# Index queries of a sparse-attention layer projected and scored from position 64 on, with the first block's scores on 64 partitions

## The chip, the cores and the metric

One core of a Trainium2 chip runs the whole kernel in one launch. The metric is the device time of an execution in microseconds (us). Each engine has a queue of its own and works through it in order: TensorE (PE, with PEld for its weight loads), VectorE (DVE), ScalarE (ACT), GpSimd (POOL), and SyncE (SP), which issues transfers.

## The reference, cut to what matters

Two layers, each a token mixer and a gated MLP, over 256 positions of width 2048. Group B of the mixer is sparse attention: 16 index heads of 64 score the keys, and each query keeps the 64 best causal keys (`top_k` is 64 here).

```
q_idx = apply_rope(q_idx.reshape(bsz, s, IDX_HEADS, IDX_DIM), icos, isin)
top_k = min(INDEX_TOPK, s // 4)
...
    dots = jnp.einsum('bthd,bsd->bths', qi_b, k_idx, preferred_element_type=jnp.float32) * (IDX_DIM ** -0.5)
    index = jnp.einsum('bths,bth->bts', jax.nn.relu(dots), wi_b)
    index = jnp.where(visible[None], index, -jnp.inf)
    _, sel = lax.top_k(index, top_k)
    ...
    ok = (sel <= q_pos[None, :, None])[:, :, None, :]
    p = jax.nn.softmax(jnp.where(ok, logits, -jnp.inf), axis=-1)
```

A query at a position below 64 sees at most 64 keys, so it keeps all of them whatever their scores are. Group A of the mixer is a gated DeltaNet, which needs, for each layer, the inverse of unit triangular matrices built from its keys.

## The kernel before, in words

Everything is kept feature-major: a tile of x is 128 features by 256 positions. Matmuls run in fp32r with a split into a high and a low part: `X[:, k, :]` holds the high part of feature tile k in columns 0 to 255 and the low part in columns 256 to 511, and each weight chunk of 128 x 1024 is split into `hi` (ACT, L171) and `lo` (DVE, L173). Such a chunk is called a **unit** below: it holds eight feature tiles ("k tiles") of one output tile, so an output tile of an input projection takes two units. Per k tile, `mm3` issues either two matmuls (L219: hi times 512 columns; L221: lo times 256 columns) or, "folded", three of 256 columns into one half bank (L216).

A generator program interleaves the rest: after each unit of matmuls every open chain (`chain_k`, `chain_iq`, `chain_inverse` and so on) is stepped once or so, and what it issues is put into the engines' queues by the tile framework's scheduler. `lo` of a unit is issued some three units ahead of its matmuls. All of it is a fixed order at run time: an instruction that waits in DVE's queue holds up every `lo` behind it, and PE waits for `lo`.

The order of units in a layer's projections is: 8 units of a group (small columns and keys 0 to 2), keys 3 to 7, z of heads 0 and 1, **the eight index-query tiles (16 units, 128 k tiles, folded)**, z 2 to 5, the key-value latent, z 6 and 7, then v, q and attention queries by head. Counted through the program, the units' `lo` conversions of layer 0 are numbers 24 to 39 for the index queries.

Three chains matter here:

- `chain_iq(i)`: rotates an index tile of two heads (`rope`, L930 to L933), splits it (L1044 ACT, L1046 DVE), scores it against the keys with three matmuls for each block of 128 queries (L1059), takes the relu (ACT, L1061) and adds it up with the heads' weights into `idx` (DVE, L1066).
- `chain_topk`: eight rounds of max and match_replace on `idx`, then the mask `bias`.
- `chain_inverse`: once all eight heads' `LT` are written (DVE, L716), POOL issues the transfers that gather the diagonal blocks (L728, L732), then runs the first 16 steps of a substitution, each one product `Wd` (L749) and one subtraction into `BX` (L751). Steps 16 to 30 run on DVE with the same two lines; the first of them, on a product of 255 elements, is called **Wd255** below, and the last subtraction **BX31**. Then the result goes out and in through DRAM (L757, L766) and the merges for v can begin.

```
eng = nc.gpsimd if j < INV_POOL else V
eng.tensor_tensor(w, B[:, j, j + 1:32][:, :, None].to_broadcast([64, n, m]),
                   X[:, j:j + 1, 0:m].to_broadcast([64, n, m]), op=ALU.mult)
eng.tensor_tensor(X[:, j + 1:32, 0:m], X[:, j + 1:32, 0:m], w, op=ALU.subtract)
if j % IRATE == IRATE - 1:
    yield
```

Of the kernel before, what the change touches and what calls it, by code (L numbers as in the profile page):

```python
# [61 lines left out]
TOPK = 64  # L62
ROPE_THETA = 10000.0
# [9 lines left out]
# the tiles of the merges: (row block, (chunk, block, number of blocks))  # L73
# [9 lines left out]
for _n, _w in (("ident", 128), ("tri", 128), ("dmask", 128), ("bd", 128), ("cmask", 384),  # L83
               ("cos", 256), ("sin", 256), ("icos", 256), ("isin", 256), ("tcos", 128), ("tsin", 128)):
    CST[_n] = (_o, _o + _w)
    _o += _w
# [8 lines left out]
class Trunk:  # L95
# [161 lines left out]
    def single(self, src, xs, nk, done, pre=None, urgent=False, fold=False, sums=False):  # L257
        box = {}

        def unit(c0, n):  # L260
            def mm(hi, lo):
                if c0 == 0:
                    box["acc"] = self.newacc()
                for q in range(n):
                    if sums and c0 + n == nk and q == LNQ:
                        self.st = [self.bank("st"), self.bank("st")]
                        for st in self.st:
                            self.nc.tensor.matmul(st[:, 0:2], self.ones, self.zero, start=True, stop=False,
                                                  skip_group_check=True)
                    self.mm3(box["acc"], hi, lo, q, xs(c0 + q), c0 + q == 0, c0 + q == nk - 1, fold)  # L270
# [199 lines left out]
    def ln_out(self, l):  # L470
        # the last norm
# [87 lines left out]
    def chain_small(self, l, acc):  # L559
# [11 lines left out]
        # log decay and beta  # L571
# [14 lines left out]
        V.tensor_scalar(self.widx, tok[:, :, 80:96], 1.0 / 32, None, op0=ALU.mult)  # L586
        yield
# [20 lines left out]
        # cumulative decays  # L608
# [29 lines left out]
        # E[j, i] = exp(gc_i - gc_j) for i >= j  # L638
# [81 lines left out]
    def chain_inverse(self, l):  # L720
# [3 lines left out]
        # diagonal 32-blocks to one block a partition  # L724
# [8 lines left out]
        # the second chunk's blocks above the diagonal into the first one's room below it  # L733
# [4 lines left out]
        # norms of k  # L738
# [186 lines left out]
    def rope(self, dst, u, cosn, sinn):  # L925
        nc = self.nc
        V = nc.vector
        t = self.m256("rt")
        sn = self.c(sinn)
        V.tensor_tensor(t[0:64], u[64:128], sn[64:128], op=ALU.mult)  # L930
        V.tensor_tensor(t[64:128], u[0:64], sn[0:64], op=ALU.mult)  # L931
        V.tensor_tensor(dst, u, self.c(cosn), op=ALU.mult)
# [99 lines left out]
    def chain_iq(self, l, i, acc):  # L1032
        nc = self.nc
        V = nc.vector
        if FOLD & 2:
            u = acc[:, 0:256]
        else:
            u = yield from self.evac(acc, self.m256("u"))
            yield
        q = self.m256("iq")  # L1040
        self.rope(q, u, "icos", "isin")
        yield
        qh = self.m256("qh").bitcast(F32R)
        nc.scalar.activation(qh, q, AF.Copy)  # L1044
        ql = self.m256("ql").bitcast(F32R)
# [4 lines left out]
        for b in range(2):  # L1050
            n = P * (b + 1)
            o = (0, P)[b]
            for _ in range(YPD if b == 0 else YPD2):
                yield
            pd = self.bank("pd")
            pdv = pd[:, 0:2 * n].rearrange("p (w s) -> p w s", w=2)
            bs = slice(b * P, (b + 1) * P)
# [3 lines left out]
            nc.scalar.activation(rl[:, 0:2 * n], pd[:, 0:2 * n], AF.Relu)  # L1061
            yield
            for w in range(2):
                hh = 2 * i + w
                prev = self.c("cmask")[:, o:o + n] if i == 0 and w == 0 else self.idx[:, o:o + n]
                V.scalar_tensor_tensor(self.idx[:, o:o + n], rl[:, w * n:(w + 1) * n], self.widx[:, b, hh:hh + 1],  # L1066
                                       prev, op0=ALU.mult, op1=ALU.add)
# [5 lines left out]
    def chain_topk(self, l):  # L1073
# [11 lines left out]
        V.tensor_scalar(self.bias, self.idx, MARK, -NEG, op0=ALU.is_equal, op1=ALU.mult)  # L1085
        V.scalar_tensor_tensor(self.bias, self.bias, NEG, self.c("cmask"), op0=ALU.add, op1=ALU.add)
# [52 lines left out]
    def plan_layer(self, l):  # L1139
# [38 lines left out]
        for i in range(8):  # L1178
            nxt(lambda acc, i=i: sp(self.chain_iq(l, i, acc)), 2)
# [111 lines left out]
def _constants():  # L1291
# [12 lines left out]
    put("cmask", np.concatenate([cm, np.zeros((P, P)), cm], 1))  # L1304

# [94 lines left out]
```

## Time and profile before

| | us |
|---|---|
| Runs, median of 3 | 2493.53 (2491.78 to 2494.53) |
| Span of the profiled execution | 2492.8 |
| PE busy in it | 2441.6 (98%) |
| DVE busy | 1934.6 (78%) |
| ACT busy | 1236.9 (50%) |
| POOL busy | 285.5 (11%) |

The span runs from the first to the last instruction; the profiled execution has no other time of its own on record, so the span stands for it. PE's busy time counts overlapping matmuls once and includes their pipeline, so 98% doesn't mean that nothing can be gained on it. Layer 0's projections lie in the first 380 us, layer 1's between about 1240 and 1650 us; the two MLPs lie between and behind.

### The profile page before, as it was taken

How to read it: one execution, taken by the hardware profiler on the slowest of the kernel's cores; microseconds unless marked ns; L12 is line 12 of the kernel's file. 1: busy time of each engine (PE TensorE's matmuls, PEld its weight loads, DVE VectorE, ACT ScalarE, POOL GpSimd, SP SyncE). 2: the span in 40 equal slices, each digit the busy share in tenths (PEclk: the TensorE clock that was granted, in tenths of full speed). 3: DMA queues.
4: the chain of work that ended last, by engine and by line, in shares of the span. 5: the costliest groups of instructions: out<-in, count | busy, mean ns of one | idle time of the engine just before them, and what ended most of it. 6: DMA issues, size and time to landing. Idle time of an engine off the chain costs nothing.

```text
span 2492.8 us, 40103 instructions
## 1 busy us (share of the span) xinstructions
PE 2441.6 (98%) x15016; PEld 2171.0 (87%) x15016; DVE 1934.6 (78%) x3769; ACT 1236.9 (50%) x2137; POOL 285.5 (11%) x377
## 2 busy tenths in 40 slices
PE   9999999999999999999999999999999999999997
PEld 9997888898888888888899888888888888888886
DVE  7789988798888887555589798887888888875555
ACT  5445666454444444444354456664544444444443
POOL 0133101320000000000233221024100000000001
PEclk9999999999999999999999999999999999999998
DMA  7554445465555555666555644454555555555664
GB/s 243 182 172 135 137 147 159 150 196 186 187 191 188 188 187 188 185 186 188 158 189 160 174 133 130 152 163 150 193 187 190 188 189 186 190 186 182 187 187 133
DMA packets 135778, 436.29 MB, mean 175 GB/s; under 512 B 26624, under 2 KB 26912, under 8 KB 135328
## 3 DMA queue, kind: packets, MB, share of 16 engines
q1 hardware_dynamic: 134272, 429.14, 54.1%
q0 software_dynamic: 1312, 4.61, 0.7%
q8 instruction: 117, 1.92, 0.3%
q14 instruction: 77, 0.63, 0.1%
HBM read 429.61 MB, written 3.69 MB: 174 GB/s over the span
## 4 chain that ended last, share of the span: by engine, by line
PE 82%; DVE 12%; DMA 2%; issue 1%; ACT 1%; POOL 1%; SPq 0%; ACTq 0%; DVEq 0%; POOLq 0%
PE acc L219 46%; PE acc L221 24%; PE acc L216 6%; DVE lo L173 4%; PE acc L241 3%; DVE y L520 1%; DMA raw<-w_in 1%; ACT hi L171 1%; DMA G<-gd 1%; DVE YB L302 1%; POOL BX L751 0%; DVE rt L931 0%; DVE idx L1083 0%; PE pd L1059 0%; DVE idx L1066 0%
## 5 line engine op out<-in xcount | busy, mean ns | idle before, releaser
L219 PE MATMUL acc<-X,hi 128*128 128x512 f32 x4000 | 1418.3, 396 | 0.0
L173 DVE TENSOR_TENSOR lo<-raw,hi 128x1024 fp32r<-128x1024 f32 (+1 forms) x821 | 993.6, 1211 | 430.5 <-ACT hi L171 428.4
L171 ACT ACTIVATE hi<-raw 128x1024 fp32r<-128x1024 f32 (+1 forms) x821 | 853.7, 1040 | 868.9 <-PE acc L219 527.2
L221 PE MATMUL acc<-X,lo 128*128 128x256 f32 x4000 | 1121.7, 280 | 4.3 <-DVE lo L173 4.3
L219 PEld LDWEIGHTS acc<-X,hi 128*128 128x128 f32 x4000 | 751.1, 188 | 173.7
L221 PEld LDWEIGHTS acc<-X,lo 128*128 128x128 f32 x4000 | 751.3, 188 | 7.1 <-DVE lo L173 6.5
L219 PE MATMUL acc<-H,hi 128*128 128x512 f32 x1320 | 466.9, 396 | 0.0
L221 PE MATMUL acc<-H,lo 128*128 128x256 f32 x1320 | 372.2, 282 | 0.0
L219 PEld LDWEIGHTS acc<-H,hi 128*128 128x128 f32 x1320 | 248.0, 188 | 60.2
L216 PE MATMUL acc<-X,hi 128*128 128x256 f32 x1408 | 259.6, 284 | 0.6 <-ACT hi L171 0.6
L221 PEld LDWEIGHTS acc<-H,lo 128*128 128x128 f32 x1320 | 247.9, 188 | 0.1
L216 PEld LDWEIGHTS acc<-X,hi 128*128 128x128 f32 x1408 | 220.1, 190 | 2.1 <-ACT hi L171 0.8
L216 PE MATMUL acc<-X,lo 128*128 128x256 f32 x704 | 200.9, 285 | 9.1 <-DVE lo L173 9.1
L216 PEld LDWEIGHTS acc<-X,lo 128*128 128x128 f32 x704 | 133.4, 189 | 10.4 <-DVE lo L173 10.3
L376 POOL COPY racc<-xT 128x256 f32<-128x256 f32 x4 | 2.1, 527 | 1043.6 <-DVE xT L374 1043.6
L390 POOL TENSOR_TENSOR racc<-racc,xT 128x256 f32<-128x256 f32 x56 | 54.9, 981 | 496.8 <-DVE xT L386 496.7
L1255 ACT ACTIVATE sq<-y 128x256 f32<-128x256 f32 x88 | 36.7, 417 | 138.3 <-DVE y L520 138.2
L313 DVE TENSOR_TENSOR u<-acc,c 128x256 f32<-128x256 f32 x232 | 96.3, 418 | 0.3
L520 DVE SCALAR_TENSOR_TENSOR vT<-u,pv,vT 128x255 f32<-128x255 f32 (+1 forms) x176 | 85.1, 483 | 5.9
L520 DVE SCALAR_TENSOR_TENSOR y<-u,fw,y 128x255 f32<-128x255 f32 (+1 forms) x176 | 84.5, 480 | 2.9
L311 ACT ACTIVATE c<-acc 128x256 f32<-128x256 f32 x232 | 84.0, 366 | 4.6 <-PE acc L221 4.6
L241 PE MATMUL acc<-X,hi 128*128 128x256 f32 x512 | 78.1, 295 | 1.9 <-ACT hi L171 1.6
(324 smaller groups left out, 2136.7 us busy)
## 6 DMA issues: line engine op xcount, KB each, us to landing
raw<-w_up SPq DMA_DIRECT2D x336, 512.0 KB, 3.7
raw<-w_in SPq DMA_DIRECT2D x188, 512.0 KB, 3.7
raw<-w_down SPq DMA_DIRECT2D x160, 512.0 KB, 3.6
raw<-w_out SPq DMA_DIRECT2D x48, 512.0 KB, 3.7
raw<-w_out_g SPq DMA_DIRECT2D x16, 512.0 KB, 3.6
raw<-w_up_g SPq DMA_DIRECT2D x16, 512.0 KB, 4.1
raw<-w_down SPq DMA_DIRECT2D x32, 256.0 KB, 3.5
raw<-w_in_g SPq DMA_DIRECT2D x15, 512.0 KB, 4.6
```

Of the source, the lines that this page charges most:

```text
L171: nc.scalar.activation(u.hi[:, o:e], u.raw[:, o:e], AF.Copy)
L173: self.pin(nc.vector.tensor_tensor(u.lo[:, o:e], u.raw[:, o:e], u.hi[:, o:e].bitcast(F32), op=ALU.subtract))
L216: nc.tensor.matmul(acc[:, 0:256], w[:, j * P:(j + 1) * P], xs[:, o:o + 256], start=first and n == 0, stop=last and n == 2)
L219: nc.tensor.matmul(acc[:, 0:512], hi[:, j * P:(j + 1) * P], xs[:, 0:512], start=first, stop=last, skip_group_check=True)
L221: nc.tensor.matmul(acc[:, 256:512], lo[:, j * P:(j + 1) * P], xs[:, 0:256], start=False, stop=last, skip_group_check=True)
L241: self.nc.tensor.matmul(accs[f][:, 0:256], w[:, j * P:(j + 1) * P], xs(k)[:, o:o + 256], start=k == 0 and n == 0, stop=k == nk - 1 and n == 2)
L302: nc.vector.tensor_scalar(dst, src, scale, None, op0=ALU.mult)
L311: nc.scalar.activation(c, acc[:, 256:512], AF.Copy)
L313: nc.vector.tensor_tensor(u, acc[:, 0:256], c, op=ALU.add)
L390: nc.gpsimd.tensor_tensor(self.racc[:, 0, :], self.racc[:, 0, :], x, op=ALU.add)
L520: nc.vector.scalar_tensor_tensor(y[:, s:256], u[:, 0:256 - s], w[:, nt - 1 - s:nt - s], y[:, s:256], op0=ALU.mult, op1=ALU.add)
L1255: nc.scalar.activation(th, y, AF.Tanh)
```

## The change

Index queries for positions 0 to 63 are neither projected nor scored. `mm3` gets a start position `t0`; with it a k tile takes two matmuls, the high weights on columns 64 to 255 of both halves (384 columns) and the low weights on 192 columns. This replaces the folded form in the index tiles, so the two halves lie apart in the bank and `chain_iq` first copies one half (ACT) and adds it to the other (DVE), with a step between. Rotation and split work on 192 columns. The first block's scores (positions 64 to 127) lie on partitions 0 to 63, with a mask `cmaskq` and weights `widx0` moved there; the rounds of the top-k run on 64 partitions for that block, and `bias` is built in five operations instead of two, back on partitions 64 to 127. Constants grow by 128 columns.

```diff
-    def mm3(self, acc, hi, lo, j, xs, first, last, fold=False):
-        nc = self.nc
+    def mm3(self, acc, hi, lo, j, xs, first, last, fold=False, t0=0):
+        nc = self.nc
+        if t0:
+            nc.tensor.matmul(acc.rearrange("p (s t) -> p s t", s=2)[:, :, t0:256], hi[:, j * P:(j + 1) * P],
+                             xs.rearrange("p (s t) -> p s t", s=2)[:, :, t0:256], start=first, stop=last,
+                             skip_group_check=True)
+            nc.tensor.matmul(acc[:, 256 + t0:512], lo[:, j * P:(j + 1) * P], xs[:, t0:256], start=False, stop=last,
+                             skip_group_check=True)
+            return
...
+        self.widx0 = self.mp.tile([P, 16], F32, name="widx0")
+        V.tensor_scalar(self.widx0[0:P - Q0], tok[Q0:P, 0, 80:96], 1.0 / 32, None, op0=ALU.mult)
...
-        if FOLD & 2:
-            u = acc[:, 0:256]
-        else:
-            u = yield from self.evac(acc, self.m256("u"))
-            yield
-        q = self.m256("iq")
-        self.rope(q, u, "icos", "isin")
-        yield
-        qh = self.m256("qh").bitcast(F32R)
+        n0 = 256 - Q0
+        c = self.t256("c", 4)[:, 0:n0]
+        nc.scalar.activation(c, acc[:, 256 + Q0:512], AF.Copy)
+        yield
+        u = self.m256("u")[:, 0:n0]
+        V.tensor_tensor(u, acc[:, Q0:256], c, op=ALU.add)
+        yield
+        q = self.m256("iq")[:, 0:n0]
+        self.rope(q, u, "icos", "isin", Q0)
+        yield
+        qh = self.m256("qh").bitcast(F32R)[:, 0:n0]
...
+            r = P - Q0 if b == 0 else P
...
-            pdv = pd[:, 0:2 * n].rearrange("p (w s) -> p w s", w=2)
-            bs = slice(b * P, (b + 1) * P)
+            pdv = pd[0:r, 0:2 * n].rearrange("p (w s) -> p w s", w=2)
+            bs = slice(0, P - Q0) if b == 0 else slice(P - Q0, 256 - Q0)
...
-            vs = [self.idx[:, 0:P], self.idx[:, P:384]]
+            vs = [self.idx[0:P - Q0, 0:P], self.idx[:, P:384]]
...
-            nxt(lambda acc, i=i: sp(self.chain_iq(l, i, acc)), 2)
+            nxt(lambda acc, i=i: sp(self.chain_iq(l, i, acc)), t0=Q0)
```

Since the scheduler sets the queues anew, other instructions move too. On DVE, in layer 0, this is the place of the first DVE step of the inverse (`Wd` is the product, `BX` the matrix that it updates, `lo` a unit's conversion, `rt`, `iq`, `ql` and `idx` belong to the index chains), before the change:

```order
L933 TENSOR_TENSOR iq<-iq,rt 128x256
L1066 SCALAR_TENSOR_TENSOR idx<-rl,widx,idx 128x256 x2
L1046 TENSOR_TENSOR ql<-iq,qh 128x256
L749 TENSOR_TENSOR Wd<-BX 64x255
L173 TENSOR_TENSOR lo<-raw,hi 128x1024
L751 TENSOR_TENSOR BX<-BX,Wd 64x15x17
L749 TENSOR_TENSOR Wd<-BX 64x252
L930 TENSOR_TENSOR rt<-acc,cst 64x256
```

In the changed kernel the same place on DVE reads (line numbers are some 11 higher):

```order
L1058 TENSOR_TENSOR ql<-iq,qh 128x192
L175 TENSOR_TENSOR lo<-raw,hi 128x1024
L1050 TENSOR_TENSOR u<-acc,c 128x192
L760 TENSOR_TENSOR Wd<-BX 64x255
L762 TENSOR_TENSOR BX<-BX,Wd 64x15x17
L760 TENSOR_TENSOR Wd<-BX 64x252
L940 TENSOR_TENSOR rt<-u,cst 64x192
L762 TENSOR_TENSOR BX<-BX,Wd 64x14x18
L941 TENSOR_TENSOR rt<-u,cst 64x192
L942 TENSOR_TENSOR iq<-u,cst 128x192
L760 TENSOR_TENSOR Wd<-BX 64x247
L175 TENSOR_TENSOR lo<-raw,hi 128x1024
```

What moved: counted from the program's start, Wd255 stood behind 44 `lo` conversions and now stands behind 40; in layer 1 it stood behind 453 and now stands behind 450. BX31 stood behind 51 and 459, and now stands behind 48 and 458. The norm step of the same chain, just behind the last `LT`, stood behind 34 and 444 and now stands behind 32 and 442.

On PE, this is a piece of the index tiles of layer 0 before the change, around a score matmul (`pd`):

```order
L216 MATMUL acc<-X,hi 128x256
L1059 MATMUL pd<-pair_1116,qh 128x256
L1059 MATMUL pd<-pair_1117,qh 128x256
L1059 MATMUL pd<-pair_1116,ql 128x256
L216 MATMUL acc<-X,hi 128x256
L216 MATMUL acc<-X,lo 128x256
L216 MATMUL acc<-X,hi 128x256 x2
```

And in the changed kernel, around the first score matmul of a 64-query block on PE:

```order
L217 MATMUL acc<-X,hi 128x2x192
L220 MATMUL acc<-X,lo 128x192
L1072 MATMUL pd<-pair_1098,qh 64x256
L1072 MATMUL pd<-pair_1099,qh 64x256
L1072 MATMUL pd<-pair_1098,ql 64x256
L217 MATMUL acc<-X,hi 128x2x192
```

What moved: two matmuls, of 384 and 192 columns, stand where three of 256 stood, and the scores keep their columns but write 64 partitions.

## Rows read from the trace of the kernel before

**Rows 1.** The page: span, and busy time, share and instructions of PE.

```profile
span 2492.8 us, 40103 instructions
...
PE 2441.6 (98%) x15016; PEld 2171.0 (87%) x15016; DVE 1934.6 (78%) x3769; ACT 1236.9 (50%) x2137; POOL 285.5 (11%) x377
```

**Rows 2.** Timeline of PE in an index unit: start us, duration us, instruction.

```profile
126.36 0.40 PE L216 MATMUL acc<-X,hi 128*128 128x256 f32 x2
...
126.72 0.40 PE L216 MATMUL acc<-X,hi 128*128 128x256 f32 x2
```

**Rows 3.** Timeline of PE in the MLP, units not folded.

```profile
800.14 0.28 PE L221 MATMUL acc<-X,lo 128*128 128x256 f32 x1
800.26 0.39 PE L219 MATMUL acc<-X,hi 128*128 128x512 f32 x1
800.49 0.28 PE L221 MATMUL acc<-X,lo 128*128 128x256 f32 x1
```

**Rows 4.** Timeline of PE: attention logits, plain fp32, two passes a matmul.

```profile
235.89 0.39 PE L1106 MATMUL pl<-ak,iq 128*128 128x128 f32 x2
236.11 0.60 PE L1107 MATMUL pl<-ak,iq 128*128 128x256 f32 x2
236.54 0.38 PE L810 MATMUL p<-F,us 128*128 128x128 f32 x2
```

**Rows 5.** Timeline of PE: matmuls of one moving column, each with its weights.

```profile
480.81 0.58 PE L398 MATMUL st<-inv,xT 128*128 128x1 f32 x4
481.26 0.47 PE L398 MATMUL st<-inv,sq 128*128 128x1 f32 x3
```

**Rows 6.** Timeline of POOL, layer 0: the inverse's first issue, first and last instruction.

```profile
104.86 2.60 POOL L728 DMA_DIRECT2D d<-LT  x4 [43.18 <-DVE rs_q L326]
...
118.28 0.23 POOL L749 TENSOR_TENSOR Wd<-BX 64x31 f32<-64x31 f32 x1 [6.06 <-DMA BX<-d]
...
143.82 0.80 POOL L751 TENSOR_TENSOR BX<-BX,Wd 64x256 f32<-64x256 f32 x1
```

**Rows 7.** Timeline of POOL, layer 1: its last instruction of the inverse.

```profile
1379.75 0.72 POOL L751 TENSOR_TENSOR BX<-BX,Wd 64x256 f32<-64x256 f32 x1
```

**Rows 8.** Timeline of DVE, layer 0: conversion 41, Wd255, BX31, conversion 52.

```profile
131.13 1.65 DVE L173 TENSOR_TENSOR lo<-raw,hi 128x1024 fp32r<-128x1024 f32 x1
...
145.68 0.41 DVE L749 TENSOR_TENSOR Wd<-BX 64x255 f32<-64x255 f32 x1
...
167.00 0.17 DVE L751 TENSOR_TENSOR BX<-BX,Wd 64x31 f32<-64x31 f32 x1
...
168.47 1.21 DVE L173 TENSOR_TENSOR lo<-raw,hi 128x1024 fp32r<-128x1024 f32 x1
```

**Rows 9.** Timeline of DVE, layer 1: conversion 451, Wd255, BX31.

```profile
1368.21 1.65 DVE L173 TENSOR_TENSOR lo<-raw,hi 128x1024 fp32r<-128x1024 f32 x1
...
1380.51 0.42 DVE L749 TENSOR_TENSOR Wd<-BX 64x255 f32<-64x255 f32 x1 [4.23 <-POOL BX L751]
...
1401.99 0.18 DVE L751 TENSOR_TENSOR BX<-BX,Wd 64x31 f32<-64x31 f32 x1
```

**Rows 10.** Windows: stretch, length, busy PE, PEld, DVE, ACT, POOL, clock, DMA.

```profile
104.80:144.70 39.90, 39.90 (x326) 39.48 (x325) 32.96 (x54) 15.49 (x22) 28.88 (x40) 1.00 0.55 167
...
82.00:104.00 22.00, 21.92 (x179) 21.22 (x178) 21.29 (x87) 8.44 (x11) 0.00 (x0) 1.00 0.50 165
```

**Rows 11.** Timeline of PE, layer 0: its idle time for `lo` behind the stretch.

```profile
147.28 0.39 PE L216 MATMUL acc<-X,lo 128*128 128x256 f32 x1 [0.35 <-DVE lo L173]
...
151.96 0.39 PE L216 MATMUL acc<-X,lo 128*128 128x256 f32 x1 [0.85 <-DVE lo L173]
```

**Rows 12.** Timeline of POOL: the same step of 60 elements, layers 0 and 1.

```profile
119.30 1.36 POOL L751 TENSOR_TENSOR BX<-BX,Wd 64x60 f32<-64x60 f32 x1
...
1357.03 0.38 POOL L751 TENSOR_TENSOR BX<-BX,Wd 64x60 f32<-64x60 f32 x1
```

**Rows 13.** Groups by line: one rotation product over 256 columns on DVE.

```profile
L932 DVE TENSOR_TENSOR iq<-acc,cst 128x256 f32<-128x256 f32 x16 | 6.8, 423 | 0.2
```

More of the change, by code (lines that the diff above doesn't have):

```diff
@@ L62 @@
 TOPK = 64
+Q0 = TOPK
 ROPE_THETA = 10000.0
@@ L82 @@
 _o = 0
-for _n, _w in (("ident", 128), ("tri", 128), ("dmask", 128), ("bd", 128), ("cmask", 384),
+for _n, _w in (("ident", 128), ("tri", 128), ("dmask", 128), ("bd", 128), ("cmask", 384), ("cmaskq", 128),
                ("cos", 256), ("sin", 256), ("icos", 256), ("isin", 256), ("tcos", 128), ("tsin", 128)):
@@ L255, in group, with single @@
         self.units.extend(unit(c) for c in range(nk // kk))
-    def single(self, src, xs, nk, done, pre=None, urgent=False, fold=False, sums=False):
+    def single(self, src, xs, nk, done, pre=None, urgent=False, fold=False, sums=False, t0=0):
         box = {}
@@ L269, in mm @@
                                                   skip_group_check=True)
-                    self.mm3(box["acc"], hi, lo, q, xs(c0 + q), c0 + q == 0, c0 + q == nk - 1, fold)
+                    self.mm3(box["acc"], hi, lo, q, xs(c0 + q), c0 + q == 0, c0 + q == nk - 1, fold, t0)
                     if q % SUB == SUB - 1 or q == n - 1:
@@ L922, in chain_q, with rope @@
         self.flags.add(("g", h))
-    def rope(self, dst, u, cosn, sinn):
-        nc = self.nc
-        V = nc.vector
-        t = self.m256("rt")
-        sn = self.c(sinn)
+    def rope(self, dst, u, cosn, sinn, t0=0):
+        V = self.nc.vector
+        t = self.m256("rt")[:, 0:256 - t0]
+        sn = self.c(sinn)[:, t0:256]
         V.tensor_tensor(t[0:64], u[64:128], sn[64:128], op=ALU.mult)
         V.tensor_tensor(t[64:128], u[0:64], sn[0:64], op=ALU.mult)
-        V.tensor_tensor(dst, u, self.c(cosn), op=ALU.mult)
+        V.tensor_tensor(dst, u, self.c(cosn)[:, t0:256], op=ALU.mult)
         V.tensor_tensor(dst, dst, t, op=ALU.add)
@@ L1034, in chain_iq @@
         V = nc.vector
-        if FOLD & 2:
-            u = acc[:, 0:256]
-        else:
-            u = yield from self.evac(acc, self.m256("u"))
-            yield
-        q = self.m256("iq")
-        self.rope(q, u, "icos", "isin")
-        yield
-        qh = self.m256("qh").bitcast(F32R)
+        n0 = 256 - Q0
+        c = self.t256("c", 4)[:, 0:n0]
+        nc.scalar.activation(c, acc[:, 256 + Q0:512], AF.Copy)
+        yield
+        u = self.m256("u")[:, 0:n0]
[5 more added lines that the diff above has]
+        qh = self.m256("qh").bitcast(F32R)[:, 0:n0]
         nc.scalar.activation(qh, q, AF.Copy)
-        ql = self.m256("ql").bitcast(F32R)
+        ql = self.m256("ql").bitcast(F32R)[:, 0:n0]
         V.tensor_tensor(ql, q, qh.bitcast(F32), op=ALU.subtract)
@@ L1060, in chain_iq @@
             rl = self.m512("rl")
-            nc.scalar.activation(rl[:, 0:2 * n], pd[:, 0:2 * n], AF.Relu)
+            nc.scalar.activation(rl[0:r, 0:2 * n], pd[0:r, 0:2 * n], AF.Relu)
             yield
@@ L1064, in chain_iq @@
                 hh = 2 * i + w
-                prev = self.c("cmask")[:, o:o + n] if i == 0 and w == 0 else self.idx[:, o:o + n]
-                V.scalar_tensor_tensor(self.idx[:, o:o + n], rl[:, w * n:(w + 1) * n], self.widx[:, b, hh:hh + 1],
-                                       prev, op0=ALU.mult, op1=ALU.add)
+                mask = self.c("cmaskq")[0:r] if b == 0 else self.c("cmask")[:, o:o + n]
+                prev = mask if i == 0 and w == 0 else self.idx[0:r, o:o + n]
+                wi = self.widx0[0:r, hh:hh + 1] if b == 0 else self.widx[:, b, hh:hh + 1]
+                V.scalar_tensor_tensor(self.idx[0:r, o:o + n], rl[0:r, w * n:(w + 1) * n], wi, prev,
+                                       op0=ALU.mult, op1=ALU.add)
             self.nidx += 1
@@ L1077, in chain_topk @@
         for r in range(TOPK // 8):
-            vs = [self.idx[:, 0:P], self.idx[:, P:384]]
-            ms = [self.small("m8", 8, 4) for _ in vs]
+            vs = [self.idx[0:P - Q0, 0:P], self.idx[:, P:384]]
+            ms = [self.small("m8", 8, 4)[0:v.shape[0]] for v in vs]
             for m8, v in zip(ms, vs):
@@ L1084, in chain_topk @@
             yield
-        V.tensor_scalar(self.bias, self.idx, MARK, -NEG, op0=ALU.is_equal, op1=ALU.mult)
-        V.scalar_tensor_tensor(self.bias, self.bias, NEG, self.c("cmask"), op0=ALU.add, op1=ALU.add)
+        b = self.bias
+        V.tensor_scalar(b[Q0:P, 0:P], self.idx[0:P - Q0, 0:P], MARK, -NEG, op0=ALU.is_equal, op1=ALU.mult)
+        V.tensor_scalar(b[:, P:384], self.idx[:, P:384], MARK, -NEG, op0=ALU.is_equal, op1=ALU.mult)
+        V.tensor_copy(b[0:Q0, 0:P], self.c("cmask")[0:Q0, 0:P])
+        V.scalar_tensor_tensor(b[Q0:P, 0:P], b[Q0:P, 0:P], NEG, self.c("cmask")[Q0:P, 0:P], op0=ALU.add, op1=ALU.add)
+        V.scalar_tensor_tensor(b[:, P:384], b[:, P:384], NEG, self.c("cmask")[:, P:384], op0=ALU.add, op1=ALU.add)
         self.flags.add("topk")
@@ L1167, in plan_layer, with nxt @@
         f = 0
-        def nxt(done, fold=0):
+        def nxt(done, fold=0, t0=0):
             nonlocal f
-            self.single(a["w_in"][l][f], xs, KT, done, fold=bool(FOLD & fold))
+            self.single(a["w_in"][l][f], xs, KT, done, fold=bool(FOLD & fold), t0=t0)
             f += 1
@@ L1304, in _constants @@
     put("cmask", np.concatenate([cm, np.zeros((P, P)), cm], 1))
+    put("cmaskq", np.concatenate([cm[Q0:], cm[:Q0]]))
     def table(dim):
```

## The prediction, put on record before the changed kernel ran

> **What bounds the kernel now.** First the page: PE is busy for 98% of a span of 2492.8 us [rows 1], so a matmul that is left out should count one for one, unless something else ends last where it stands. The index tiles take 128 k tiles a layer, 256 in all. PE's timeline there gives their price: from one pair of hi matmuls to the next 0.36 us pass, 126.36 to 126.72 [rows 2]; that is a folded k tile, three matmuls of 256 columns. Next I asked who else is busy around these units. In layer 0 between 82 and 104 us, where their first ones run, DVE is busy 21.29 of 22 us [rows 10]: it writes the eight heads' `LT`. From there a second chain runs beside PE. POOL issues the inverse's first transfer at 104.86, waits for its blocks until 118.28 and works to 143.82 + 0.80 = 144.62 [rows 6]: 39.8 us. DVE reaches Wd255, which needs POOL's last result, at 145.68 [rows 8], one microsecond later. In layer 1 POOL ends at 1380.47 [rows 7], and there DVE stood idle for it, 4.23 us before Wd255 at 1380.51 [rows 9]. So in this stretch POOL's chain is as long as PE's work, and DVE's queue ties the two together: a `lo` behind Wd255 can't start before POOL is done, and PE can't go on without `lo`.
>
> **The matmuls.** A k tile loses three matmuls of 256 columns and gets one of 384 and one of 192. At full rate 256 columns take 0.12 us (800.14 to 800.26) and 512 take 0.23 [rows 3]; 384 lie halfway, 0.175. For 192 fp32r columns there is no row: every fp32r matmul of this kernel moves at least 256. From below the price is bounded by the weight load that each matmul brings: matmuls of a single column follow each other in 0.11 us (480.81 to 481.26 for four) [rows 5]. From above it is bounded by the four-byte matmuls that run without fp32r's rate: plain fp32 on 256 columns takes 0.43 us (236.11 to 236.54, the x2 being its two passes) [rows 4], so 192 columns take 192/256 x 0.43 = 0.32. Of plain fp32, 128 columns take 0.22 (235.89 to 236.11), again 1.7 ns a column. The k tile then costs 0.285 or 0.495 us against 0.36: over 128 k tiles a layer gains 9.6 us or loses 17.3, both layers -19.2 or +34.6.
>
> I take the upper end. Both ends are far, and the choice is a judgement: the only four-byte matmuls under 256 columns that the trace has cost as much a column as the slow form, and none shows the fast rate there. TensorE: Matmul & The Clock Gate in the Trainium skill (section Back-to-back issue gap) speaks against that: it lets the spacing grow with the column count alone, 2.5 ns on top, and names no lower limit for a type. By it the k tile is at the lower end and the sum on PE is -19.2 us. The trace agrees with it for 256 and 512 columns within some 8% [rows 3], and no row shows it below.
>
> **What of the loss is covered.** 34.6 us is on PE, which is the bound where nothing else is. Taken off: layer 1's 4.23 us of DVE waiting for POOL [rows 9], which a later PE meets anyway; layer 0's idle 0.35 and 0.85 us of PE [rows 11]; and part of the first two index tiles, which run where DVE is full [rows 10]: their 32 k tiles lose 4.3 us a layer, of which I take 1 us a layer as hidden. That leaves 34.6 - 4.2 - 1.2 - 2 = 27.2.
>
> **The moved wait.** Wd255 moves up in DVE's queue by four conversions in layer 0 and three in layer 1, so conversions 41 and 451 now lie behind it. With the slow matmuls this costs nothing: conversion 41, at 131.13 today [rows 8], would come at 131.13 + 17.3 = 148.4 by PE's pace, and POOL ends at 144.62 with some 2.9 us of DVE work (eight instructions at about 0.36) ahead of it, 147.5. PE's loss is the cover; without it, the wait is the next section's first rival.
>
> **The rest.** In a chain of an index tile, DVE gets one addition more and its five other full-width operations shrink from 256 to 192 columns; at no more than 0.423 us for 256 [rows 13] the sum lies between +0.4 and below nothing, so I take nothing. ACT gets eight small copies a layer and is busy 15.49 of 39.9 us there [rows 10]: hidden. The copy and its steps make each chain some steps longer; what waits for `idx` is the top-k, far behind. The score matmuls keep their columns, so halving the stationary side could save at most part of a load that already runs ahead. `bias` takes three operations more, up to 1.3 us of DVE a layer at 0.423 each, or nothing where DVE has room: I take 0.5. Larger constants are one transfer's worth of a few per cent at the start: nothing.
>
> Sum: 27.2 + 1 = 28.2 us. On the profiled execution's 2492.8 that is 2521.0; the median of the runs is 0.7 us above the span, which gives **2521.7 us**. Its own range is 2513 (half of the index loss hidden) to 2529 (none hidden, 34.6 + 1).
>
> **Rivals.**
>
> *The fast matmul, and the wait decides* (chance 0.30). If 192 columns run at the lower price, PE gains 9.6 us a layer, and all of it meets POOL's chain. Wd255 then waits until 144.62, and conversion 41 starts at about 147.5 instead of 131.13, 16.4 us late; in layer 1 conversion 451 starts at 1380.47 + 2.9 instead of 1368.21, 15.2 us late. Part comes back: DVE's half of the inverse ends with POOL's end, at 167.17 as today [rows 8], and by then three conversions fewer have been done. Conversions 41 to 52 come every (168.47 - 131.13)/11 = 3.4 us [rows 8], so 10.2 us stay; in layer 1, with one fewer behind BX31 at 1401.99 [rows 9], 3.4. Bounds +13.6 and +31.6; nearer the lower, because what follows hangs on the inverse's end: +18, or 2511.5. So it is slower by either price of the matmul. The GPSIMD Engine Reference of the Trainium skill (section Specifications, on SBUF interfaces) says that POOL shares these with DVE when DVE reads two inputs. By that rule a DVE that stands still would let POOL finish sooner, and this rival would lose less. The trace agrees so far: one step of 60 elements took 1.36 us in layer 0 and 0.38 in layer 1 [rows 12].
>
> *Faster* (0.08). The fast matmul, and POOL's chain shrinks enough that Wd255 finds it done: 2492.8 + 0.7 - 19.2 = 2474. Between the chain's start and Wd255 lie eight conversions, at 8 x 0.285 = 2.3 us of PE each some 18 us, with small matmuls perhaps 24, against 39.8 us of chain. It decides only if the chain falls below that, and of its 39.8 us POOL works in 28.88 [rows 10] and waits for transfers in the rest; taking 1 us off each of ten steps is not enough.
>
> *No change* (0.05). A price between the two ends, or the second rival with POOL faster, so that shifts cancel: 2489 to 2498.
>
> *Much slower* (0.03). The 384 columns, being two pieces of 192, run slowly too: 384/256 x 0.43 = 0.645, the k tile 0.965, +0.605 x 256 = 155 us: 2648.
>
> **How the numbers follow.** The forecast has 0.54, the rivals 0.30, 0.08, 0.05 and 0.03. 2521.7 is the likeliest case's time. From 2503 (the second case with a faster POOL) to 2533 (the first with nothing hidden and some of the wait on top) about 0.80 lie; out are the faster, unchanged and much slower ones and the low tail of the wait. Less than 0.2% (5 us) a measurement of this kernel can hardly tell from no change. Faster by more: 0.08; within: 0.05; slower: 0.87, the sum of the cases that end there.
>
> **What would show it.** In PE's timeline of the changed kernel, from one 384-column matmul to the 192-column one behind it: 0.175 us; from there to the next: 0.32 if I am right, 0.11 to 0.12 if the first rival is. In DVE's waits, Wd255 for POOL: under 2 us a layer if right, 8 us and more in each layer in the first rival, with conversion 41 right behind it. The stretch from the first index unit to the units of z behind it should be some 17 us longer a layer, and the MLPs unchanged. I am wrong if the 192 columns are cheap, if POOL's 39.8 us shrink by ten and more, or if DVE's longer index chains delay `lo` in the full stretch around 82 to 104 us.

## The result and the profile after

The changed kernel takes 2512.31 us (median of 4 runs, 2510.24 to 2515.19), the kernel before 2492.67 beside it (2491.78 to 2494.53): ratio 1.008, 95% interval 1.0068 to 1.0092. It is 19.6 us slower. The time is within the range on record (2503 to 2533), just under the range of the forecast's own case (2513 to 2529), and on its side of zero, but the matmuls did the opposite of what the forecast supposed: TensorE's work became smaller, as in its first rival.

The page of the changed kernel: its span is 17.8 us longer, with 7 us less of busy PE [rows 1].

```profile
span 2510.6 us, 39632 instructions
...
PE 2434.7 (97%) x14760; PEld 2162.3 (86%) x14760; DVE 1934.1 (77%) x3793; ACT 1238.0 (49%) x2153; POOL 279.9 (11%) x377
```

PE's timeline in the index units of layer 0 (start us, duration us, instruction, in brackets the idle time before it and what ended it):

```profile
109.37 0.36 PE L217 MATMUL acc<-X,hi 128*128 128x384 f32 x1
...
109.66 0.36 PE L217 MATMUL acc<-X,hi 128*128 128x384 f32 x1
109.85 0.25 PE L220 MATMUL acc<-X,lo 128*128 128x192 f32 x1
109.94 0.36 PE L217 MATMUL acc<-X,hi 128*128 128x384 f32 x1
...
110.23 0.36 PE L217 MATMUL acc<-X,hi 128*128 128x384 f32 x1
...
124.28 0.53 PE L220 MATMUL acc<-X,lo 128*128 128x192 f32 x1 [1.92 <-DVE lo L175]
124.60 0.58 PE L217 MATMUL acc<-X,hi 128*128 128x384 f32 x1
124.98 0.36 PE L220 MATMUL acc<-X,lo 128*128 128x192 f32 x1
125.14 0.58 PE L217 MATMUL acc<-X,hi 128*128 128x384 f32 x1
...
142.85 0.58 PE L225 MATMUL acc<-X,lo 128*128 128x256 f32 x1 [4.61 <-DVE lo L175]
```

The 384 columns take 0.19 to 0.20 us and the 192 columns 0.09; three k tiles in a row, 109.37 to 110.23, give 0.287 each, against 0.36 [rows 2]. That is 256 x 0.073 = 18.7 us less on PE. The same k tile takes 0.54 us at 124.60: there the granted clock is at its lower level (0.50 between 124 and 130 us, 1.2 GHz), and PE's busy time falls by 7 us in all, not by 18.7. The windows over the two stretches of [rows 10] show what became of the saving (stretch, length, busy PE, PEld, DVE, ACT, POOL, clock, DMA share, GB/s):

```profile
82.00:104.00 22.00, 18.06 (x118) 17.32 (x117) 20.41 (x95) 6.83 (x12) 2.42 (x4) 0.92 0.43 133
104.80:144.70 39.90, 30.56 (x172) 29.04 (x171) 30.08 (x56) 12.15 (x23) 22.27 (x35) 0.78 0.47 137
```

PE was never idle in the second stretch before; now it stands still for 9.3 of its 39.9 us and the granted clock there falls from 1.00 to 0.78. PE's waits of the changed kernel between 60 and 200 us name the cause (us in total, times, longest):

```profile
PE acc L220 <- DVE lo L175: 5.7, 6, 1.9
PE acc L225 <- DVE lo L175: 4.6, 1, 4.6
PE pm L716 <- DVE LT L727: 3.5, 2, 3.4
```

PE waits for `lo`. The 4.6 us are the conversion behind Wd255; the other waits for `lo`, 5.7 us in six, lie ahead of Wd255, in the index units themselves. Between 82 and 104 us PE stands still for 3.9 us, all of it for DVE's `LT` and `pair`, none for `lo`. DVE's timeline, conversion 40, Wd255 and conversion 41 of layer 0, then Wd255 and conversion 451 of layer 1, answers to [rows 8, 9]:

```profile
131.08 1.72 DVE L175 TENSOR_TENSOR lo<-raw,hi 128x1024 fp32r<-128x1024 f32 x1
132.72 0.34 DVE L1050 TENSOR_TENSOR u<-acc,c 128x192 f32<-128x192 f32 x1
138.45 0.42 DVE L760 TENSOR_TENSOR Wd<-BX 64x255 f32<-64x255 f32 x1 [5.38 <-POOL BX L762]
...
141.59 1.21 DVE L175 TENSOR_TENSOR lo<-raw,hi 128x1024 fp32r<-128x1024 f32 x1
...
1388.60 0.42 DVE L760 TENSOR_TENSOR Wd<-BX 64x255 f32<-64x255 f32 x1 [8.19 <-POOL BX L762]
...
1391.74 1.21 DVE L175 TENSOR_TENSOR lo<-raw,hi 128x1024 fp32r<-128x1024 f32 x1
```

Wd255 waits 5.38 and 8.19 us for POOL. Conversion 41 starts 10.5 us later than before, conversion 451 23.5 us, of which 7.9 are layer 0's loss (below) and 15.6 layer 1's own. POOL's chain itself was a little shorter in layer 0 (first issue, first product, last step; 36.8 us against 39.8 in [rows 6]):

```profile
101.58 0.68 POOL L739 DMA_DIRECT2D d<-LT  x1 [38.37 <-DVE rs_q L335]
...
115.47 0.23 POOL L760 TENSOR_TENSOR Wd<-BX 64x31 f32<-64x31 f32 x1 [5.71 <-DMA BX<-d]
...
137.69 0.72 POOL L762 TENSOR_TENSOR BX<-BX,Wd 64x256 f32<-64x256 f32 x1
```

Between the layers the loss stands at 8 us: conversion 400 starts at 1199.17 before and at 1207.10 after. The other 10 us come in layer 1's mixer. There PE's wait for the conversion behind Wd255 is no longer than before, 6.1 us in both kernels; what is new between 1290 and 1460 us are chiefly PE's waits for `lo` in the index units (3.9 us), for ACT's `hi` (3.1) and for `LT` (1.9). The layers' other parts are unchanged (PE busy for 935.1 and 934.6 us between 250 and 1190; the loss is 8.0 us at conversion 100 already).

### The profile page after: what moved, and what is told of

Its sections match the earlier page's. It is cut to its first block, busy times and chain, and to the rows that moved or that the text cites. A ratio compares the mean times of both kernels' runs of the same rounds, so it can differ in the third digit from the quotient of the medians.

```text
span 2510.6 us, 39632 instructions
## 1 busy us (share of the span) xinstructions
PE 2434.7 (97%) x14760; PEld 2162.3 (86%) x14760; DVE 1934.1 (77%) x3793; ACT 1238.0 (49%) x2153; POOL 279.9 (11%) x377
## 5 line engine op out<-in xcount | busy, mean ns | idle before, releaser
L230 PE MATMUL acc<-X,lo 128*128 128x256 f32 x4000 | 1121.8, 280 | 0.0
L228 PEld LDWEIGHTS acc<-X,hi 128*128 128x128 f32 x4000 | 751.2, 188 | 173.5
L230 PEld LDWEIGHTS acc<-X,lo 128*128 128x128 f32 x4000 | 751.6, 188 | 0.5
L225 PE MATMUL acc<-X,hi 128*128 128x256 f32 x896 | 166.2, 286 | 0.0
L225 PEld LDWEIGHTS acc<-X,hi 128*128 128x128 f32 x896 | 141.4, 192 | 0.6
L225 PE MATMUL acc<-X,lo 128*128 128x256 f32 x448 | 128.4, 287 | 11.9 <-DVE lo L175 11.9
L225 PEld LDWEIGHTS acc<-X,lo 128*128 128x128 f32 x448 | 86.3, 193 | 12.6 <-DVE lo L175 12.6
L217 PE MATMUL acc<-X,hi 128*128 128x384 f32 x256 | 85.5, 392 | 3.1 <-ACT hi L173 3.1
```

The lines of the kernel that those rows point to most:

```text
L217: nc.tensor.matmul(acc.rearrange("p (s t) -> p s t", s=2)[:, :, t0:256], hi[:, j * P:(j + 1) * P], xs.rearrange("p (s t) -> p s t", s=2)[: ...
```

## The experiments

Three theories had to be told apart. **A**: the place of Wd255 in DVE's queue costs the time. **B**: between the index units and the inverse DVE is too full to convert in time for a faster PE, wherever Wd255 stands. **C**: the copy (ACT) and the add (DVE) that join the two accumulator halves cost it. The kernel before ran at 2488.8 to 2490.0 us beside these runs, so all are given as differences to it (an expectation that gives times counts from 2492.7); the changed kernel's own is +19.6. "At 43, 453" means that Wd255 stands in DVE's queue behind so many conversions, counted from the kernel's start (before: 44, 453; changed: 40, 450). The one trace of the kernel before is the first session's, 2492.8 us, some 4 us longer than beside the later runs, so spans and start times across traces compare no better than that.

**Wd255 held back.**

```diff
             w = self.m256("Wd")[0:64, 0:n * m].rearrange("p (n m) -> p n m", n=n)
+            if j == INV_POOL:
+                for _ in range(3):
+                    yield
             eng = nc.gpsimd if j < INV_POOL else V
```

> The changed kernel with three more pauses of the inverse's chain just ahead of its first DVE step (Wd255), which puts that step behind conversion 43 of layer 0 and 453 of layer 1 (40 and 450 in the changed kernel, 44 and 453 in the kernel before); all else is the changed kernel's. Theory A (the place of Wd255 costs the time: it waits 5.4 and 8.2 us for POOL's chain and the conversions behind it wait with it): the 13.6 us of waits and some of what follows them go, so 2490 to 2499 us. Theory B (DVE is too full between the position-sliced units and the inverse to convert in time for the faster PE, wherever Wd255 stands): TensorE goes on waiting for conversions, 2504 to 2513 us.

Measured 2499.47 us against 2488.79, +10.7 (ratio 1.0044, 1.0029 to 1.0059). Wd255 no longer waits in either layer. A had -3 to +6, B +11 to +20: the hold gives back 8.9 of the 19.6 us, so A holds for a little under half, and neither theory for all of it. The windows of this run show where the rest is:

```profile
118.00:124.00 6.00, 4.01 (x25) 3.76 (x25) 5.44 (x12) 2.68 (x5) 5.04 (x12) 0.93 0.36 118
124.00:130.00 6.00, 4.29 (x22) 3.89 (x22) 5.86 (x11) 2.23 (x5) 5.37 (x9) 0.78 0.31 105
130.00:136.00 6.00, 2.44 (x14) 2.17 (x12) 5.92 (x8) 1.53 (x3) 5.45 (x8) 0.79 0.19 66
```

The same windows of the kernel before:

```profile
118.00:124.00 6.00, 6.00 (x53) 6.00 (x52) 3.04 (x4) 2.39 (x3) 5.01 (x10) 1.00 0.51 178
124.00:130.00 6.00, 6.00 (x50) 5.86 (x49) 5.89 (x10) 2.91 (x4) 5.37 (x9) 1.00 0.57 172
130.00:136.00 6.00, 6.00 (x53) 6.00 (x52) 5.96 (x8) 2.69 (x4) 5.53 (x7) 1.00 0.28 94
```

Held back, DVE is busy for 17.2 of these 18 us and PE for 10.7, ahead of Wd255 (148.0). Before, PE was busy for all 18 and DVE for 14.9; from 124 us on DVE was just as full, and PE did not wait. DVE's timeline of the held kernel shows what stands between one conversion and the next:

```profile
124.06 0.34 DVE L1053 TENSOR_TENSOR u<-acc,c 128x192 f32<-128x192 f32 x1
124.44 0.35 DVE L943 TENSOR_TENSOR rt<-u,cst 64x192 f32<-64x192 f32 x1
124.81 0.55 DVE L944 TENSOR_TENSOR rt<-u,cst 64x192 f32<-64x192 f32 x1
125.39 0.57 DVE L945 TENSOR_TENSOR iq<-u,cst 128x192 f32<-128x192 f32 x1
126.00 0.55 DVE L946 TENSOR_TENSOR iq<-iq,rt 128x192 f32<-128x192 f32 x1
126.47 1.60 DVE L175 TENSOR_TENSOR lo<-raw,hi 128x1024 fp32r<-128x1024 f32 x1
```

An add, a whole rotation, then the conversion: from one `lo` (120.94) to the next 5.5 us, while a unit of eight k tiles takes PE 8 x 0.287 = 2.3. The kernel before has one gap as long (5.4 us from 125.72), but from 116.38 to 137.05 its conversions start every 3.4 us on average, in the held kernel from 115.77 to 135.16 every 4.8. PE also waits for ACT's `hi` in the held kernel, 1.9 us in layer 0 and 3.1 in layer 1 (0.6 and none before). By the traces the loss that is left is layer 0's: 5.8 us at conversion 400 and 5.1 at conversion 500, although layer 1 has the same copy and add; why stays open.

**The old units with an early Wd255.** The kernel before, with one line changed:

```diff
-            if j % IRATE == IRATE - 1:
+            if j % IRATE == IRATE - 1 and j not in (5, 7, 9, 11, 13, 15):
```

> The kernel before with the pauses between POOL's steps 5 to 15 of the inverse left out, so that Wd255 stands behind conversion 42 of layer 0 and 451 of layer 1 instead of 44 and 453; the projection and the scoring are those of before. Theory A: Wd255 now waits for POOL's chain, about 4 us in layer 0 and 7 in layer 1, and the time rises by 8 to 18 us to 2501 to 2511. Theory B: the old units are slow enough for DVE to catch up, 2490 to 2497 us.

Measured 2509.31, +20.5 (1.0085, 1.007 to 1.01), just above A's +8 to +18. Wd255, two conversions earlier in the queue, waits 9.1 and 11.1 us, and the loss is as large as that of the whole change, with the old projection and scoring. (POOL's steps move up too: in layer 0 they end at 139.91 us, before at 144.62.) DVE's waits in layer 1 (1290 to 1460 us) of this run:

```profile
DVE Wd L749 <- POOL BX L751: 11.1, 1, 11.1
```

and PE's in layer 0 (60 to 200 us):

```profile
PE acc L216 <- DVE iq L932: 9.3, 2, 9.2
```

Not only conversions stand behind Wd255: a rotation (`iq`, L932) does too, and it frees an accumulator that PE needs. So B's claim that the old, slower units leave DVE room is wrong where the queue's order is bad.

**Three matmuls of 192 columns, no copy and no add.**

```diff
-            nc.tensor.matmul(acc.rearrange("p (s t) -> p s t", s=2)[:, :, t0:256], hi[:, j * P:(j + 1) * P],
...
+            for n, (w, o) in enumerate(((hi, t0), (hi, 256 + t0), (lo, t0))):
+                nc.tensor.matmul(acc[:, t0:256], w[:, j * P:(j + 1) * P], xs[:, o:o + 256 - t0], start=first and n == 0,
+                                 stop=last and n == 2)
...
-        c = self.t256("c", 4)[:, 0:n0]
-        nc.scalar.activation(c, acc[:, 256 + Q0:512], AF.Copy)
-        yield
-        u = self.m256("u")[:, 0:n0]
-        V.tensor_tensor(u, acc[:, Q0:256], c, op=ALU.add)
-        yield
+        u = acc[:, Q0:256]
```

> The changed kernel with the projection of positions 64 to 255 as three matmuls of 192 columns into one accumulator (hi x hi, hi x lo, lo x hi), so that ACT's copy and DVE's add of each head pair are gone; Wd255 stays at 40 and 450. PE's k tile becomes about 0.33 us (three loads of 0.11) instead of 0.288, at most 256 x 0.042 = 10.8 us more on PE. Theory A: the waits of Wd255 stay, the DVE work saved lies beside them, 2504 to 2516 us. Theory B: DVE is relieved of sixteen adds and ACT of sixteen copies in the full stretch, so the units' conversions come earlier, 2494 to 2503 us. Theory C (the copy and the add themselves are the loss): 2490 to 2496 us.

Measured 2496.80, +8.0 (1.0032, 1.002 to 1.0044), in B's range (+1 to +10) and out of those of A (+11 to +23) and C (-3 to +3): 11.6 us better than the changed kernel, although its k tile is longer on PE (0.34 us, timeline below) and Wd255 stands as early as there. But Wd255 waits less: POOL's chain starts and ends earlier (in layer 0 97.37 to 133.26 us, 101.58 to 138.41 in the changed kernel), and the waits are 1.3 and 3.5 us instead of 5.4 and 8.2. So this run does not part the copy and the add from the wait.

**All columns projected again, the rest as changed.** The branch with `t0` in `mm3` is taken out, so the units run as matmuls of 512 and 256 columns.

```diff
-        if t0:
-            nc.tensor.matmul(acc.rearrange("p (s t) -> p s t", s=2)[:, :, t0:256], hi[:, j * P:(j + 1) * P],
...
-            return
```

> The changed kernel with the first 64 positions projected again (matmuls of 512 and 256 columns, 0.35 us a k tile instead of 0.288, 256 x 0.06 = 15 us more on PE), and the rest of the chain on positions 64 to 255 as changed; Wd255 falls back to 44 and 453 with it. Theory A with PE's saving real: the waits go (-14 to -18) and the saving goes (+15), 2508 to 2515 us. Theory B (DVE sets the pace of this stretch, so that PE's saving is worth nothing): the saving costs nothing to give up and the waits go, 2495 to 2502 us.

Measured 2498.92, +10.1 (1.0043, 1.0026 to 1.006). PE's timeline of it, 0.35 us a k tile:

```profile
109.68 0.39 PE L221 MATMUL acc<-X,hi 128*128 128x512 f32 x1
109.92 0.28 PE L223 MATMUL acc<-X,lo 128*128 128x256 f32 x1
110.03 0.39 PE L221 MATMUL acc<-X,hi 128*128 128x512 f32 x1
```

That is 1 us above B's range and well under A's. With Wd255 at 44 and 453 it is as fast as the held kernel, whose PE has 256 x 0.063 = 16 us less to do. B's point: with the copy and the add in the chain, PE's saving in these units is worth nothing that can be measured.

**Fold and hold together.** Both edits above.

> The changed kernel with the projection of positions 64 to 255 as three matmuls of 192 columns into one accumulator (no copy and no add) and with three more pauses ahead of Wd255, which puts it at 43 and 453. In differences to the kernel before on the same chip: the fold alone left +8.0 us, with PE waiting 3.3 and 4.9 us for the first conversion behind the inverse's start. Theory A+B (the place of Wd255 and DVE's extra steps add up): both removed, -3 to +2 us. Theory A alone (the place is all, the fold helped only through it): the pauses give again what they gave the changed kernel, -9, so about -1, and the rest cannot be told from A+B; if the two overlap, the pauses give little here, +4 to +8 us.

Measured 2485.07 against 2488.80, -3.7 us (0.9982, 0.9973 to 0.9991; 11 runs): just under the range for both causes adding up; A alone, with about -1 expected, is not excluded by this run. The pauses gave 11.7 us here, no less than without the fold and more than the 4.8 us of waits of Wd255 that they take away, and this version is faster than both kernels. Its page, and its PE timeline in an index unit:

```profile
span 2482.8 us, 40109 instructions
...
PE 2433.6 (98%) x15016; PEld 2163.2 (87%) x15016; DVE 1938.2 (78%) x3777; ACT 1234.9 (50%) x2137; POOL 289.9 (12%) x377
```

```profile
109.83 0.28 PE L218 MATMUL acc<-X,lo 128*128 128x192 f32 x1
109.94 0.39 PE L218 MATMUL acc<-X,hi 128*128 128x192 f32 x2
110.17 0.27 PE L218 MATMUL acc<-X,lo 128*128 128x192 f32 x1
```

A k tile takes 0.34 us, 0.02 less than before; 256 of them are 5 us, near what was gained; that the gain comes from there no run shows. (The span is 10 us under [rows 1], but beside this run the kernel before took 2488.80.)

**Hold, without the copy and the add, matmuls as changed.** From the held kernel:

```diff
-        c = self.t256("c", 4)[:, 0:n0]
-        nc.scalar.activation(c, acc[:, 256 + Q0:512], AF.Copy)
-        yield
-        u = self.m256("u")[:, 0:n0]
-        V.tensor_tensor(u, acc[:, Q0:256], c, op=ALU.add)
-        yield
+        u = acc[:, Q0:256]
```

> The changed kernel with the three pauses (Wd255 at 43 and 453) and without ACT's copy and DVE's add of the index projection: the chain reads the first accumulator half alone and leaves out the products that the other half holds; TensorE's matmuls stay as changed (0.288 us a k tile). With the copy and the add this was +10.7 us against the kernel before. Theory B (DVE is what is full here): relieving DVE of 16 adds gives back 5 to 10 us, so 0 to +6 us, and PE's shorter tiles show no gain of their own (not under -3). Theory that PE's pace decides once DVE's adds are gone: the 18 us that TensorE saves appear, -8 to -18 us. If the adds are hidden: +9 to +12 us.

Measured 2488.22, -0.6 us (0.9996, 0.9987 to 1.0005), just under B's range (0 to +6). The copy and the add are worth 10.7 + 0.6 = 11.3 us here, the whole rest of the loss, and still nothing of PE's 18.7 us comes to light. DVE's full queue is not the only reason: at the same place, 43 and 453, Wd255 waits for POOL again (layer 0, then layer 1):

```profile
DVE Wd L763 <- POOL BX L765: 3.6, 1, 3.6
...
DVE Wd L763 <- POOL BX L765: 2.8, 1, 2.8
```

With the chain shorter DVE reaches Wd255 at 139.84 us, 8.1 earlier than in the held kernel, and POOL's chain is not done. So part of PE's saving runs into POOL's chain, as the prediction's first rival said; what a later place of Wd255 would give here was not run. The same windows as above, of this run:

```profile
118.00:124.00 6.00, 4.83 (x32) 4.70 (x33) 4.91 (x9) 3.16 (x6) 5.22 (x11) 1.00 0.47 162
124.00:130.00 6.00, 5.04 (x36) 4.57 (x35) 5.92 (x10) 2.30 (x4) 5.53 (x7) 1.00 0.48 139
130.00:136.00 6.00, 5.28 (x42) 4.93 (x41) 5.39 (x8) 1.66 (x4) 5.45 (x7) 1.00 0.46 163
```

PE is busy for 15.1 of the 18 us instead of 10.7 and keeps its clock, but it still idles for 2.9 us where the kernel before had no idle time, and DVE is busy for 16.2.

**The copy and the add alone**, at full width, in the kernel before:

```diff
-FOLD = 11
+FOLD = 9
```

> The kernel before with one constant changed: the index queries are projected by two matmuls of 512 and 256 columns with ACT's copy and DVE's add of 256 columns, for all positions, scoring as before; Wd255 comes to 45 and 454. It measures the copy and the add alone. Theory B: they load DVE where it is full and cost 6 to 12 us, as in the run with all columns and the new scoring (+10.1 us). Theory A (only the place of Wd255 costs): 0 to +4 us.

Measured 2497.58, +8.8 by the medians (1.003, 1.0021 to 1.0039): in B's range. Wd255 waits 1.0 us in layer 1 and not at all in layer 0, so its place is no part of this loss. But B's way is not what the trace shows: PE waits less for `lo` than before (0.7 and 4.0 us in the two layers, 2.0 and 8.3 before), and instead for the chains, 2.4 us for `qh` and 0.7 for `ql` in layer 0, and for accumulators freed late (1.7 us behind `zs`, 2.4 behind `pair`). This points to the length of the chain itself; no run shows it alone.

**The scoring alone.** The projection of the kernel before, without the copy and the add (as in the diff above), the chain behind it as changed.

```diff
-            nxt(lambda acc, i=i: sp(self.chain_iq(l, i, acc)), t0=Q0)
+            nxt(lambda acc, i=i: sp(self.chain_iq(l, i, acc)), 2)
```

> The scoring alone: the changed kernel with the projection of the kernel before (three matmuls of 256 columns into one accumulator, all positions), while rope, scores, top-k and bias work on positions 64 to 255 as changed; Wd255 comes to 43 and 452. Theory A: one conversion earlier in each layer, a wait of 1 to 4 us in each, +2 to +6 us. Theory B: DVE does slightly less (shorter rope steps, 64 partitions), so -4 to +1 us.

Measured 2495.47, +6.7 (1.0026, 1.0015 to 1.0037), just above A's range; Wd255 at 43 and 452 waits 1.3 and 7.1 us, where A had 1 to 4 in each layer. Then the same with two pauses ahead of Wd255 (`range(2)` in the hold's diff):

> The scoring alone (projection of the kernel before, all positions, no copy and no add; rope, scores, top-k and bias on positions 64 to 255) with two pauses ahead of Wd255, which puts it at 44 and 453, where the kernel before has it. Without them it was +6.7 us, with waits of Wd255 of 1.3 and 7.1 us. Theory A (that run lost by the place alone): -2 to +2 us. If the work on 64 partitions itself costs: +4 to +7 us.

Measured 2490.79 against 2489.51, +1.3 (1.0008, 0.9999 to 1.0017): with Wd255 at its old place the work on 64 partitions costs nothing that can be measured. Theory A holds for this part alone.

**Fold and hold, the whole inverse later.**

```diff
-IWAIT = 2
+IWAIT = 4
```

> The version with three matmuls of 192 columns, no copy, no add and three pauses ahead of Wd255 (-3.7 us against the kernel before), with two more pauses ahead of the whole inverse, POOL's steps too: Wd255 at 45 and 455. If the place in it is still early for a step of the inverse that holds conversions up, it gains again, -5 to -9 us; if the waits are gone already (no wait of Wd255 in its trace), the place no longer decides: -2 to -5 us; if the merges behind the inverse now come late, 0 to +5 us.

Measured 2488.84, -0.7 (0.9999, 0.999 to 1.0008), between the ranges for "the place no longer decides" and for the merges coming late. No wait of Wd255 is left in either version, and a later inverse gave most of the gain away; what comes late in its place stays open.

**A steadier PE.** The held kernel, its hi matmul on 512 columns.

```diff
-            nc.tensor.matmul(acc.rearrange("p (s t) -> p s t", s=2)[:, :, t0:256], hi[:, j * P:(j + 1) * P],
-                             xs.rearrange("p (s t) -> p s t", s=2)[:, :, t0:256], start=first, stop=last,
+            nc.tensor.matmul(acc[:, 0:512], hi[:, j * P:(j + 1) * P], xs[:, 0:512], start=first, stop=last,
```

> The changed kernel with the three pauses (Wd255 at 43 and 453) and with the hi matmul of the index tiles on all 512 columns again (0.235 instead of 0.198 us), the lo matmul on 192: a k tile of about 0.32 us against 0.288, some 8 us more on PE in all; the first 64 positions' sums are not read. With 384 columns this was +10.7 us against the kernel before, with the granted clock at 0.50 to 0.98 in half of the 6-us stretches of layer 0 between 76 and 142 us. If the clock's fall is what the copy and the add cost (PE idles in lumps, then works at half rate): a steadier PE keeps its clock and it is +3 to +8 us. If the clock's fall only fills time in which PE would wait for conversions anyway: +9 to +13 us, whether the clock stays up or not. If PE's pace decides: +17 to +20 us.

Measured 2501.23 against 2489.97, +11.3 (1.0045, 1.0028 to 1.0062). The expectation's k tile was too short: from 110.64 to 110.98 us it takes 0.34 us, not 0.32, so PE gets some 14 us more, not 8 (busy 2442.3 us, 2428.3 in the held kernel). The windows of this run that answer to the held kernel's:

```profile
118.00:124.00 6.00, 6.00 (x36) 5.20 (x36) 4.98 (x12) 2.54 (x6) 2.81 (x8) 1.00 0.55 173
124.00:130.00 6.00, 5.36 (x31) 4.39 (x31) 5.63 (x11) 2.02 (x4) 5.44 (x8) 1.00 0.27 94
130.00:136.00 6.00, 2.65 (x15) 1.83 (x13) 4.85 (x8) 2.47 (x4) 5.38 (x8) 1.00 0.23 83
```

The clock stays at 1.00 in these windows, where the held kernel had 0.93, 0.78 and 0.79, and some 14 us of work are added to PE: the time stays where it was. PE is busy for 14 us more and nothing is lost, so PE's pace does not decide in the held kernel. That the lower clock cost nothing there, because it only filled time in which PE would have waited for conversions, is the expectation's reading of +9 to +13 and is not shown: in this run the clock fell elsewhere (0.50 between 76 and 82 us, as in the held kernel, and 0.72 between 136 and 142), and over the whole execution it is the same (0.988, 0.987 in the held kernel).

The four kernels with and without each of the two edits:

| us against before | Wd255 at 40, 450 | at 43, 453 |
|---|---|---|
| matmuls of 384 and 192, copy and add | +19.6 | +10.7 |
| three matmuls of 192, no copy, no add | +8.0 | -3.7 |

The later place is worth 8.9 and 11.7 us, the form without copy and add 11.6 and 14.4. Only the 14.4 are free of waits of Wd255, which neither kernel of that column has; in the first column these waits differ too (13.6 and 4.8 us).

## Why the prediction was right in time and wrong in cause

**The price of the matmul: "I take the upper end."** This is the step that failed. 192 fp32r columns take 0.09 us, not 0.32, and the k tile 0.287, at the lower end (0.285), so PE's term is -18.7 us instead of +34.6, and "what of the loss is covered" and the cover of the moved wait fall with it. With this term reversed, 28.2 us forecast and 19.6 measured agree by luck. The formula of TensorE: Matmul & The Clock Gate in the Trainium skill (section Back-to-back issue gap), by which the gap grows with the column count alone, held against the slow price: no slow form appeared. Worked out from it the pair of 384 and 192 would take 0.245 us and the three of 256 before 0.328, so 21 us less over 256 k tiles, estimates all; the prediction's -19.2 "by it" is the sum of its own lower prices. The trace shows 0.287 and 0.36. The section gives it for a matmul by itself and says that in a stream of weight loads and matmuls both set the spacing, which the prediction left out; the three matmuls of 192 columns agree with that, at 0.11 us each where the formula gives 0.083, an estimate. The plain fp32 rows [rows 4] were the wrong neighbours for an fp32r matmul.

**The moved wait.** The places were right, and "with the slow matmuls this costs nothing" lost its condition. The rival forecast conversion 41 to be 16.4 us late (10.5 measured) and 451 15.2 (15.6 measured, without the 7.9 that layer 0 hands on), with a wait of 8 us and more in each layer (5.4 and 8.2). POOL did finish sooner while DVE stood still, as the rival allowed: its last six steps took 4.3 us (134.09 to 138.41), before, beside a working DVE, 5.7 (138.88 to 144.62). Its result, 2511.5, lies 0.8 us from the measured time, but that is luck too, for it explains only half of the loss: the held kernel is still 10.7 us slower than before.

**"The rest": "so I take nothing".** This is the second wrong term. The addition and the copy were set against the shorter rotations and found free. As busy time that came out: an addition of 0.35 us, five operations some 0.07 shorter each, and DVE busy for 1934.1 us against 1934.6. What the step left out is where this work stands and that the chain is two steps longer: the copy and the add cost 11 to 14 us with the faster units, and about 8 in the kernel before. The profile held a warning: DVE was busy for 21.29 of 22 us where the chains start [rows 10], and for 11.9 of the 12 us between 124 and 136. How the 11 to 14 us divide between DVE's time, ACT's copy ahead of `hi`, the handover from ACT to DVE and the two more pauses in each chain stays open: no run took one of them alone. For `bias` and the scoring the step was right: 1 us in the sum, +1.3 measured with an interval that includes zero.

**"A matmul that is left out should count one for one, unless something else ends last where it stands."** The condition decided. In the held kernel DVE is busy for 17.2 of 18 us while PE idles for 7.3 of them, and even without copy and add 18.7 us less on PE gave 0.6, with Wd255 waiting for POOL again (3.6 and 2.8 us).

**The signs it named.** From the 192-column matmul to the next: 0.09, on the rival's side of 0.11 to 0.12 and below it, so the 0.11 us of [rows 5] was no lower bound. From 384 to 192: 0.175 forecast, 0.19 to 0.20 measured. Each layer longer by some 17 us: 8 and 10 instead. MLPs unchanged: yes. Its last sentence, that it is wrong "if DVE's longer index chains delay `lo` in the full stretch", did not come true there: between 82 and 104 us PE waited for `LT` and `pair`, 3.9 us, and not for `lo`. `lo` came late at 116 to 136 us, beside POOL's chain.

## What to carry to other kernels

Before a saving on the busiest engine is counted, look at the engine that feeds it in the same stretch: here DVE needed 5.5 us from one conversion to the next where PE would have needed 2.3, and the saving became idle time. Then look at the next chain that the faster engines will meet: without the copy and the add it was POOL's. In a queue with a fixed order, a change to the chains also moves every instruction that waits for another engine; three places in DVE's queue were worth 9 to 12 us, one place 5, two places 20 in the kernel before, so check the place of such instructions first and pin it before judging the change itself. Choose the form of the saving that adds no step on the feeder: three matmuls of 192 columns into one accumulator save 5 us on PE instead of 19, and with Wd255 held back they are the ones that made the kernel faster.

## What the runs showed of the hardware

fp32r matmuls of 192 columns run near the rate of the wider ones, and show no slow form: alternating with 384 columns, 0.09 us to the next; three in a row, 0.34 us, so 0.11 each, the spacing of one-column matmuls [rows 5]. The pair has 576 columns in 0.287 us, the three have the same 576 in 0.34. A pair of 512 and 192 takes 0.34 to 0.35 (110.64 to 110.98 in the last run), hardly less than 512 and 256 (0.35). A conversion on DVE takes 1.72 us at 131.08, while POOL works, and 1.21 at 141.59, once POOL is done. That fits what the GPSIMD Engine Reference of the Trainium skill (section Specifications) says of SBUF interfaces that POOL and DVE share. PE's granted clock went to its lower level (0.50, 1.2 GHz) in stretches where it waited for `lo` (1.92 us at 124.28), and a k tile took 0.54 us instead of 0.287.
